# Sixteen more rows of expert products beside the making of gates, parked in DRAM, and gate sums two groups behind their one-hots

## The chip, the cores and the metric

One core of one Trainium2 chip runs the whole program. The metric is the device time of one execution in microseconds (us); lower is better. TensorE (PE) does the matrix products, VectorE (DVE), ScalarE (ACT) and GpSimd (POOL) the rest; SyncE (SP), ACT and POOL issue DMAs.

## The reference

Two transformer blocks run one after the other on 512 tokens of width 1024. The change lies in the last part of the second, a mixture of 16384 experts (128 x 128 keys), of which each token takes 128 (8 heads x 16):

```
sc = einsum(q, subkeys); vals, ids = top_k(sc, 16)          # two halves per head
cand = vals0 + vals1;  top, pos = top_k(cand, 16);  idx = expert numbers
g = softmax(top)
u = u_tab[idx]; a = einsum('chkd,cd->chk', u, x)            # 128 per token
wgt = g * gelu(a)
out = einsum('chk,chkd->cd', wgt, v_tab[idx])
```

## The kernel before, in words

The first 128 tokens take their experts by gathering rows of `u_tab` and `v_tab` (`gather`: 256 indirect DMAs of 512 KB issued by POOL, one long DVE operation for each). The other 384 tokens (`ND`) go through all 16384 experts densely, in 128 rows of 128 experts:

- `ustep(r)` makes row r of the first product: 24 matmuls of 128 x 384 over the transposed table `put`, in three terms of split precision, then a gelu on ACT into a slot of X, a ring of 38 slots in SBUF (`xrow`).
- `vstep(r)` multiplies row r by its gates (`gmul`), splits it in a high and a low part (`gmul`, `split`) and adds it into six PSUM banks by 18 matmuls of 128 x 512 over `pv`.
- Weights come as 512 KB tiles `wraw` on SP's queue, three buffers; ACT casts the high part `whi`, DVE subtracts the low part `wlo` (`wsplit`), one row ahead.

The gates of the 384 tokens are made before any `vstep` can run. `choice` yields small pieces of work, each with a cost: for each block of 128 tokens `chosen` and `weigh` (top 16 of the candidates, softmax, transposes), then `gates_of`: 16 groups of 8 tokens. A group is four DVE operations (two one-hots `o2`, `wh`, two products `wl`, `wh`) and two sums; a sum is 8 fp16 products of 128 x 128 on PE into a bank and one ACT copy into `sg`. Three sums fill an `sg` tile of 12 tokens (two buffers), which a DMA on ACT's queue writes to the DRAM table G. G is read back 8 rows at a time on SP's queue (`ring`).

Order of the work: nothing is scheduled at run time. `LEAD` = 37 rows of `ustep` come ahead of the first `vstep`; during them each of the 8 calls of `do` in a row adds `PACE0` to a debt, and pieces of `choice` are written into the streams until their costs have paid it (`tick`). Then rows of `ustep` and `vstep` alternate (PACE1, PACE2), with the choice for the first 128 tokens and the gather as the paced work, and when `ustep` has run out `vstep` goes on alone (PACE3). In `gates_of` the sums of a group are written after the DVE operations of the next one (a list `lag` that holds one group), and the three tiles of a group have two buffers each.

Of the kernel before, what the change touches and what calls it, by code (L numbers as in the profile page):

```python
# [10 lines left out]
F32 = mybir.dt.float32  # L11
F32R = mybir.dt.float32r
F16 = mybir.dt.float16
I32 = mybir.dt.int32
U32 = mybir.dt.uint32
AF = mybir.ActivationFunctionType
# [13 lines left out]
ND = 384  # L30
TB = 12
NB = ND // TB
GR = 8
GS = 32768.0

NX1, NX2 = 30, 8
LEAD = 37
NLAST = 11

PACE0, PACE1, PACE2, PACE3 = 0.85, 0.27, 0.21, 0.15  # L40

C_ANW, C_FNW, C_GNW, C_CW, C_AOG, C_COG, C_CW2, C_CT, C_N1, C_N2, C_FIN, C_N = 0, 8, 16, 17, 65, 69, 73, 85, 93, 101, 109, 117
R_ALOG, R_DTB, R_FB, R_SNK, R_QG, R_KG, R_IF, R_N = 0, 4, 8, 16, 24, 88, 152, 184
# [85 lines left out]
class Kern:  # L129
# [61 lines left out]
    def weights(self):  # L191
        a = self.a
        w = [a["wi"][i] for i in range(12)]
        for f in range(4):
            w += [a["wi"][16 + f], a["wi"][20 + f]]
        w += [a["wi"][24 + f] for f in range(4)]
        w += [a["wi"][12 + f] for f in range(4)]
        w += [a["wo"][h, k] for h in range(2) for k in (2, 3, 0, 1)]
        w += [a["wgu"][f, i] for f in range(NFF) for i in range(2)]
        w += [a["wd"][h, k] for h in range(2) for k in range(NFF // 2)]  # L200
        w += [a["wi2q"][k] for k in range(4)]
        w += [a["wi2k"][k] for k in range(2)]
        for f in range(4):
            w += [a["wi2b"][i + f] for i in (4, 8, 0)]
        w += [a["wo2"][h, k] for c in ((2, 3), (0, 1)) for h in range(2) for k in c]
        self.lim = len(w) + 2
        w += [a["wq"][f] for f in range(16)]
        self.lov = set()
        n = len(w)
        w += [a["put"][e] for e in range(LEAD)]  # L210
        for e in range(128):
            if e + LEAD < 128:
                w.append(a["put"][e + LEAD])
            w.append(a["pv"][e * 128:e * 128 + 128])
        self.lov.update(range(n, len(w)))
        self.wl, self.wraw, self.wsp, self.wi, self.w3 = w, [], [], 0, None
# [1493 lines left out]
    def peer(self):  # L1710


        nc, tc, a = self.nc, self.tc, self.a
        V, S, G = nc.vector, nc.scalar, nc.gpsimd
        hi, lo = self.h2
        with ExitStack() as es:
# [6 lines left out]
            av = self.tl(qp, [128, 128], F32)  # L1723
            self.i1T, self.i2T, self.ghT, self.glT = [self.tl(qp, [128, ND, 2], F16) for _ in range(4)]
            iota = self.tl(qp, [128, 128], F16)
            self.G = self.tl(self.dr, [128 // GR, 128, NB, GR, TB], F32)
            ub = [self.bank("gx") for _ in range(2)]
            with tc.tile_pool(name="q1", bufs=1, side="right") as q1:
                vals = self.tl(q1, [128, 4, 16, 16], F32)
                ids = self.tl(q1, [128, 4, 16, 16], U32)  # L1730
                with tc.tile_pool(name="q2", bufs=2, side="right") as q2:
# [12 lines left out]
                    for f in range(16):  # L1744
                        p = self.first[f][0] if f < 3 else self.proj512(hi, lo, 0)
                        qT = self.tl(q2, [128, T], F32, "qT", bufs=5)
                        S.copy(qT, p)
                        if f == 3:

                            for n in range(2):  # L1750
                                pb = self.bank("pj")
                                for j in range(4):
                                    k = n * 4 + j
# [13 lines left out]
                    r0 = len(pend) - 1  # L1767
# [4 lines left out]
                q3 = gp.__enter__()  # L1772
                work = self.choice(q1, q3, vals, ids, iota)

                def tick(pace):
                    self.due += pace
                    while self.due > 0:
                        c = next(work, None)
                        self.due = self.due - c if c else -1e9
                self.chose0 = False  # L1780
                ready = False
                for r in range(r0, LEAD):
                    self.ustep(hi, lo, r, ub, lambda: tick(PACE0 if not ready else PACE1))
                    if r == LEAD - 1:
                        for _ in range(0 if ready else 10**6):
                            if next(work, None) is None:
                                break
                    if not ready and (self.due < -1e6 or r == LEAD - 1):

                        ready = True  # L1790
                        gp.__exit__(None, None, None)
                        self.due = 0.0
                        rp = es.enter_context(tc.tile_pool(name="rp", bufs=2, reuse_waits="tile"))
                        self.ring(rp, 0)
                        gat = self.gather(qp, hm, ga, av)

                        def rest():
                            yield from self.chosen(q1, 0, vals[:, 0], ids[:, 0])
                            for x in self.late:
                                yield from x  # L1800
                            self.chose0 = True
                            yield from gat
                        work = rest()
# [2 lines left out]
                self.split(rp, 0)  # L1806
                k = 0
                while not self.chose0:
                    self.ustep(hi, lo, LEAD + k, ub, lambda: tick(PACE1))
                    self.vstep(rp, k, vb, lambda: tick(PACE1))  # L1810
                    k += 1
            for k in range(k, 126):
                if k + LEAD < 128:
                    self.ustep(hi, lo, LEAD + k, ub, lambda: tick(PACE2))
                pace = PACE2 if k + LEAD < 128 else PACE3
                self.vstep(rp, k, vb, lambda: tick(pace))
                if k == 128 - NLAST:
                    self.preload()
# [1 line left out]
                pass  # L1820
            self.finish(rp, ga, vb)

    def xrow(self, r):
        s = r % (NX1 + NX2)
        return self.X[0][:, s] if s < NX1 else self.X[1][:, s - NX1]

    def ring(self, rp, g):

        if g == 0:
            self.grows = []  # L1830
        t = self.tl(rp, [128, NB, GR, TB], F32, "gt", bufs=2)
        self.nc.sync.dma_start(t, self.G[g])
        self.grows.append(t)

    def gmul(self, rp, r):
# [9 lines left out]
    def preload(self):  # L1845

        nc = self.nc
        live = {r % (NX1 + NX2) for r in range(128 - NLAST, 128)}
        self.rowf = []
# [48 lines left out]
    def ustep(self, hi, lo, r, ub, do=lambda: None):  # L1898

        p = ub[r % 2][:, :ND]  # L1900
        self.prod(p, self.nextw(), (hi, lo), slice(128, 512), 8, do)
        self.nc.scalar.activation(self.xrow(r), p, AF.Gelu_apprx_tanh)  # L1902

    def vstep(self, rp, r, vb, do):

# [42 lines left out]
    def gates_of(self, q3, t, iota):  # L1948

        nc, V, S = self.nc, self.nc.vector, self.nc.scalar  # L1950
        lag = []

        def sums(n, o2, wh, wl):
            ps = self.bank("pj")
            for j in range(4):
                o = slice(j * 128, j * 128 + 128)
                self.mm(ps[:, o], o2[:, j], wh[:, j], True, False)
                self.mm(ps[:, o], o2[:, j], wl[:, j], False, True)
            q = n * 4 % TB
            if q == 0:  # L1960
                self.stage = self.tl(q3, [128, 128, TB], F32, "sg", bufs=2)
            S.activation(self.stage[:, :, q:q + 4].rearrange("p e j -> p j e"), ps.rearrange("p (j e) -> p j e", j=4),  # L1962
                         AF.Copy, scale=1.0 / GS)
            if q + 4 == TB:
                b = n * 4 // TB
                nc.scalar.dma_start(self.G[:, :, b].rearrange("g p r t -> p g (r t)"),
                                    self.stage.rearrange("p (g r) t -> p g (r t)", r=GR))
        GT = 8
        b2 = iota.rearrange("p (a b) -> p a b", b=2).unsqueeze(1).to_broadcast([128, GT, 64, 2])
        v4 = lambda ap: ap.rearrange("p t (a b) -> p t a b", b=2)  # L1970
        for n in range((t - 1) * 16, t * 16):
            o2, wh, wl = [self.tl(q3, [128, GT, 128], F16, tag, bufs=2) for tag in ("o2", "wh", "wl")]
            bt = lambda ap: ap[:, n * GT:n * GT + GT].unsqueeze(2).to_broadcast([128, GT, 64, 2])
            V.tensor_tensor(v4(o2), b2, bt(self.i2T), op=OP.is_equal)
            yield 0.66
            V.tensor_tensor(v4(wh), b2, bt(self.i1T), op=OP.is_equal)
            yield 0.66
            V.tensor_tensor(v4(wl), v4(wh), bt(self.glT), op=OP.mult)
            yield 0.66
            V.tensor_tensor(v4(wh), v4(wh), bt(self.ghT), op=OP.mult)  # L1980
            lag.append((n, o2, wh, wl))
            for m in range(2 if len(lag) > 1 else 0):
                sums(lag[0][0] * 2 + m, *[x[:, m * 4:m * 4 + 4] for x in lag[0][1:]])
                if m == 0:
                    yield 0.66
            if len(lag) > 1:
                lag.pop(0)
            else:
                yield 0.66
        for m in range(2):  # L1990
            sums(lag[0][0] * 2 + m, *[x[:, m * 4:m * 4 + 4] for x in lag[0][1:]])

    def gather(self, qp, hm, ga, av):
        nc, a = self.nc, self.a
# [181 lines left out]
```

## Time and profile before

| | |
|---|---|
| median of 3 runs | 2405.67 us (2398.84 to 2410.49) |
| the profiled execution | 2407.29 us, its span 2405.5 us |
| busy share of the span | PE 94%, DVE 68%, ACT 37%, POOL 33% |
| mean granted TensorE clock | 0.966 of full speed |
| DMA | 438.07 MB, 182 GB/s over the span |

Busy shares are means over stages with different limits, so a change of one stage is read from rows of that stage. PE matmuls are pipelined and their ends modelled, so the time of one row of products is read from the distance between equal instructions, not from their durations. "DMA share" is the mean busy share of the 16 DMA engines; a granted clock of 1.00 is 2.4 GHz, 0.5 is 1.2 GHz.

### The profile page before, as it was taken

What the parts mean: (1) busy time and instruction counts of PE and PEld (TensorE: products, weight loads), DVE (VectorE), ACT (ScalarE), POOL (GpSimd) and SP (SyncE); (2) the same over time, 40 slices, a digit from 0 to 9 for tenths busy, and PEclk for the clock granted to TensorE, in tenths of its full rate; (3) what the DMA queues carried; (4) which work ended last, traced back from release to release, by engine and by line L of the source; (5) the groups of instructions that cost most, each with busy time, mean ns of one, the idle gap of its engine ahead of it and who ended that gap; (6) DMA issues with size and microseconds to landing.
All of it is one profiled execution on the core that took longest, in us unless ns stands there. A gap on an engine that the chain in (4) does not pass through costs nothing.

```text
span 2405.5 us, 31911 instructions
## 1 busy us (share of the span) xinstructions
PE 2257.5 (94%) x12063; PEld 1948.3 (81%) x12063; DVE 1639.1 (68%) x3031; ACT 897.0 (37%) x1386; POOL 800.8 (33%) x519
## 2 busy tenths in 40 slices
PE   7898999999999998999968678999999999999998
PEld 6888777877778876778857668899999999999887
DVE  6865345465640266775897887778888788888865
ACT  4442423332222242443327565333333333333332
POOL 3553201555554353443100000234344343434300
PEclk9899889999999999999989899999999999999999
DMA  3122100365643221122226466698999999899954
GB/s 123 56 78 73 36 1 1 123 216 195 209 162 111 88 88 53 62 105 89 75 75 184 136 189 206 237 339 321 338 326 335 321 334 328 316 325 326 344 200 161
DMA packets 186647, 438.07 MB, mean 182 GB/s; under 512 B 89215, under 2 KB 90135, under 8 KB 184317
## 3 DMA queue, kind: packets, MB, share of 16 engines
q1 hardware_dynamic: 82172, 272.79, 32.3%
q0 software_dynamic: 37312, 135.20, 16.4%
q10 hardware_dynamic: 67008, 28.05, 4.4%
q8 instruction: 94, 1.54, 0.3%
q14 instruction: 61, 0.49, 0.1%
HBM read 405.22 MB, written 30.70 MB: 181 GB/s over the span
## 4 chain that ended last, share of the span: by engine, by line
PE 74%; DVE 15%; ACT 5%; DMA 3%; issue 2%; POOL 1%; SPq 0%; ACTq 0%; DVEq 0%; POOLq 0%
PE pj L161 42%; PE gx L161 25%; PE hold L161 5%; DMA u<-sg 2%; PE gx L185 2%; DVE w L634 2%; DVE wlo L234 1%; ACT whi L232 1%; ACT sg L1962 1%; DVE w L768 1%; DVE cmu L2108 1%; DVE cmu L2103 0%; DMA wraw<-in_wi_dram 0%; POOL alo L343 0%; DVE w L632 0%
## 5 line engine op out<-in xcount | busy, mean ns | idle before, releaser
L232 ACT CAST whi<-wraw 128x1024 fp32r<-128x1024 f32 x400 | 420.1, 1051 | 342.9 <-issue 147.9
L234 POOL TENSOR_TENSOR wlo<-wraw,whi 128x1024 fp32r<-128x1024 f32 x135 | 353.2, 2618 | 380.1 <-ACT whi L232 376.0
L234 DVE TENSOR_TENSOR wlo<-wraw,whi 128x1024 fp32r<-128x1024 f32 x265 | 329.9, 1245 | 196.4 <-ACT whi L232 194.1
L161 PE MATMUL gx<-alo,whi 128*128 128x384 f32 x1024 | 352.4, 344 | 0.0
L161 PE MATMUL gx<-ahi,whi 128*128 128x384 f32 x1024 | 351.1, 343 | 0.0
L2010 POOL DMA_INDIRECT gr<-in_pu_dram,u x128 | 152.0, 1187 | 577.2 <-DVE u L2133 351.4
L161 PE MATMUL pj<-ahi,whi 128*128 128x512 f32 (+2 forms) x1000 | 321.8, 362 | 4.5 <-ACT ahi L339 4.2
L161 PE MATMUL pj<-alo,whi 128*128 128x512 f32 (+2 forms) x1000 | 313.3, 353 | 0.0
L2010 POOL DMA_INDIRECT gr<-in_pv_dram,u x128 | 157.7, 1232 | 233.3 <-DVE u L2029 174.0
L161 PE MATMUL gx<-ahi,wlo 128*128 128x384 f32 x1024 | 214.2, 349 | 18.9 <-DVE wlo L234 18.9
L161 PE MATMUL pj<-ahi,wlo 128*128 128x512 f32 (+2 forms) x1000 | 210.1, 354 | 2.2 <-DVE wlo L234 2.2
L161 PEld LDWEIGHTS pj<-ahi,whi 128*128 128x128 f32 x1000 | 176.0, 193 | 37.3 <-issue 7.5
L161 PEld LDWEIGHTS gx<-ahi,wlo 128*128 128x128 f32 x1024 | 185.1, 195 | 21.8 <-DVE wlo L234 21.8
L161 PE MATMUL pj<-whi,eh 128*128 128x512 f32 x512 | 199.9, 390 | 0.0
L161 PE MATMUL pj<-wlo,eh 128*128 128x512 f32 x512 | 199.2, 389 | 0.0
L161 PEld LDWEIGHTS gx<-ahi,whi 128*128 128x128 f32 x1024 | 196.2, 192 | 3.6
L161 PEld LDWEIGHTS gx<-alo,whi 128*128 128x128 f32 x1024 | 196.1, 191 | 3.5
L161 PEld LDWEIGHTS pj<-alo,whi 128*128 128x128 f32 x1000 | 174.9, 192 | 23.8
L161 PEld LDWEIGHTS pj<-ahi,wlo 128*128 128x128 f32 x1000 | 165.2, 192 | 29.1 <-DVE wlo L234 2.6
L1902 ACT ACTIVATE u<-gx 128x384 f32<-128x384 f32 x128 | 63.5, 496 | 320.2 <-PE gx L161 319.7
L161 PE MATMUL pj<-whi,el 128*128 128x512 f32 x512 | 179.1, 390 | 0.0
L2029 DVE SCALAR_TENSOR_TENSOR u<-gr,u,u 128x1024 f32<-128x1024 f32 x128 | 163.9, 1281 | 2.5 <-DMA gr<-in_pv_dram,u 1.6
(472 smaller groups left out, 3872.2 us busy)
## 6 DMA issues: line engine op xcount, KB each, us to landing
wraw<-in_put_dram SPq DMA_DIRECT2D x128, 512.0 KB
wraw<-in_pv_dram SPq DMA_DIRECT2D x128, 512.0 KB
nu<-in_adaw_dram SPq DMA_DIRECT2D x48, 512.0 KB
u<-sg ACTq DMA_DIRECT2D x32, 768.0 KB
gt<-u SPq DMA_DIRECT2D x16, 1536.0 KB
wraw<-in_wgu_dram SPq DMA_DIRECT2D x44, 512.0 KB
wraw<-in_wi_dram SPq DMA_DIRECT2D x28, 512.0 KB
wraw<-in_wd_dram SPq DMA_DIRECT2D x22, 512.0 KB
```

Of the source, the lines that this page charges most:

```text
L161: self.nc.tensor.matmul(out, l, r, start=start, stop=stop)
L185: self.nc.tensor.transpose(out, in_, self.ident[:n, :n])
L232: self.nc.scalar.copy(hi, raw)
L234: (self.nc.vector if i in self.lov else self.nc.gpsimd).tensor_tensor(lo, raw, hi.bitcast(F32), op=OP.subtract)
L634: V.scalar_tensor_tensor(o, pad[:, t:t + TA], cw(t), o, op0=OP.mult, op1=OP.add)
L768: V.tensor_tensor(t, X[:, 0:i, 0:i].rearrange("p j c -> p c j"), A[:, i:i + 1, 0:i].to_broadcast([np_, i, i]), op=OP.mult)
L1902: self.nc.scalar.activation(self.xrow(r), p, AF.Gelu_apprx_tanh)
L1962: S.activation(self.stage[:, :, q:q + 4].rearrange("p e j -> p j e"), ps.rearrange("p (j e) -> p j e", j=4), AF.Copy, scale=1.0 / GS)
L2010: G.indirect_dma_start(out=u, out_offset=None, in_=a[items[i][0]], in_offset=bass.IndirectOffsetOnAxis(ap=self.idx[:, items[i][1]:items[i] ...
L2029: V.scalar_tensor_tensor(ga, u, wv[:, s:s + 1], ga, op0=OP.mult, op1=OP.add)
L2108: V.tensor_tensor(x[:, :, 0:n], x[:, :, 0:n], x[:, :, n:2 * n], op=OP.add)
```

## The change

`NSP` = 16 rows are put ahead of the lead: 53 rows of `ustep` now come before the first `vstep`. The first 16 go to slots of X and from there to a DRAM tile `xd` by a DMA on ACT's queue, so that their slots serve the next rows. The order of the `vstep`s is turned by 16: rows 16 to 127 first, rows 0 to 15 last, and G is read in that order. The 16 parked rows come back by DMAs on SP's queue, one at each of the first 16 steps that have no `ustep`. The sums of a group now follow by two groups instead of one, with three buffers for its tiles, and the costs per call of `do` are lower in the lead and higher after it.

```diff
+NSP = 16
-PACE0, PACE1, PACE2, PACE3 = 0.85, 0.27, 0.21, 0.15
+PACE0, PACE1, PACE2, PACE3 = 0.56, 0.30, 0.22, 0.17
...
-        w += [a["put"][e] for e in range(LEAD)]
-        for e in range(128):
-            if e + LEAD < 128:
-                w.append(a["put"][e + LEAD])
+        w += [a["put"][e] for e in range(NSP + LEAD)]
+        for k in range(128):
+            if NSP + LEAD + k < 128:
+                w.append(a["put"][NSP + LEAD + k])
+            e = (NSP + k) % 128
             w.append(a["pv"][e * 128:e * 128 + 128])
...
+            self.xd = self.tl(self.dr, [NSP, 128, ND], F32)
...
-                for r in range(r0, LEAD):
+                for r in range(r0, NSP + LEAD):
...
             for k in range(k, 126):
-                if k + LEAD < 128:
-                    self.ustep(hi, lo, LEAD + k, ub, lambda: tick(PACE2))
-                pace = PACE2 if k + LEAD < 128 else PACE3
+                both = NSP + LEAD + k < 128
+                if both:
+                    self.ustep(hi, lo, NSP + LEAD + k, ub, lambda: tick(PACE2))
+                elif k + LEAD < 128:
+                    nc.sync.dma_start(self.xrow(k + LEAD), self.xd[NSP + LEAD + k - 128])
+                pace = PACE2 if both else PACE3
                 self.vstep(rp, k, vb, lambda: tick(pace))
...
-        self.nc.sync.dma_start(t, self.G[g])
+        self.nc.sync.dma_start(t, self.G[(g + NSP // GR) % (128 // GR)])
...
-        self.nc.scalar.activation(self.xrow(r), p, AF.Gelu_apprx_tanh)
+        x = self.xrow(r - NSP if r >= NSP else r)
+        self.nc.scalar.activation(x, p, AF.Gelu_apprx_tanh)
+        if r < NSP:
+            self.nc.scalar.dma_start(self.xd[r], x)
...
-            o2, wh, wl = [self.tl(q3, [128, GT, 128], F16, tag, bufs=2) for tag in ("o2", "wh", "wl")]
+            o2, wh, wl = [self.tl(q3, [128, GT, 128], F16, tag, bufs=3) for tag in ("o2", "wh", "wl")]
...
-            for m in range(2 if len(lag) > 1 else 0):
+            for m in range(2 if len(lag) > 2 else 0):
...
-            if len(lag) > 1:
+            if len(lag) > 2:
                 lag.pop(0)
...
-        for m in range(2):
-            sums(lag[0][0] * 2 + m, *[x[:, m * 4:m * 4 + 4] for x in lag[0][1:]])
+        for x in lag:
+            for m in range(2):
+                sums(x[0] * 2 + m, *[y[:, m * 4:m * 4 + 4] for y in x[1:]])
+                yield 0.1
```

On ACT, in the middle of the gates of the third block, before the change (`sg` is a copied sum, `u<-gx` a gelu, `whi` the cast of the next row's weights, the DMA writes an `sg` tile to G):

```order
L232 CAST whi_11384<-wraw_11185 128x1024
L1962 ACTIVATE sg_11359<-pj_11394 128x4x128
L1966 DMA u_8628<-sg_11359 128x16x96
L1962 ACTIVATE sg_11417<-pj_11408 128x4x128
L1962 ACTIVATE sg_11417<-pj_11432 128x4x128
L1962 ACTIVATE sg_11417<-pj_11445 128x4x128
L1966 DMA u_8628<-sg_11417 128x16x96
L1962 ACTIVATE sg_11478<-pj_11469 128x4x128
L1962 ACTIVATE sg_11478<-pj_11483 128x4x128
L1902 ACTIVATE u_8617<-gx_8629 128x384
L232 CAST whi_11498<-wraw_11299 128x1024
```

and with it:

```order
L1911 ACTIVATE u_8617<-gx_8630 128x384
L235 CAST whi_11397<-wraw_11282 128x1024
L1973 ACTIVATE sg_11390<-pj_11418 128x4x128
L1973 ACTIVATE sg_11390<-pj_11431 128x4x128
L1977 DMA u_8629<-sg_11390 128x16x96
L1973 ACTIVATE sg_11467<-pj_11458 128x4x128
L1911 ACTIVATE u_8617<-gx_8631 128x384
L235 CAST whi_11470<-wraw_11335 128x1024
L1973 ACTIVATE sg_11467<-pj_11482 128x4x128
L1973 ACTIVATE sg_11467<-pj_11508 128x4x128
L1977 DMA u_8629<-sg_11467 128x16x96
```

Six sums stood between two casts, now three. Over the whole lead the 96 sums stood beside 19 rows of `ustep` and now stand beside 27; of the other rows ahead of the last sum, 14 were there before (rows 0 and 1 among them), and 22 are now.

On ACT beside the first choosing, where the parked rows are made, each gelu is now followed by a DMA to `xd`:

```order
L1911 ACTIVATE u_8617<-gx_8631 128x384
L1913 DMA u_8628<-u_8617 128x384
L235 CAST whi_9947<-wraw_9857 128x1024
L2154 ACT_TABLE_LOAD
L2154 ACTIVATE ctv_9682<-ctv_9682 128x128
L1911 ACT_TABLE_LOAD
L1911 ACTIVATE u_8617<-gx_8630 128x384
L1913 DMA u_8628<-u_8617 128x384
L235 CAST whi_10002<-wraw_9906 128x1024
```

Nothing of this sort stood between a gelu and the cast behind it. On SP, from the first `vstep` without a `ustep`, with the change (`gt` is the read of G):

```order
L1821 DMA u_8617<-u_8628 128x384
L224 DMA wraw_18374<-in_pv_dram 128x1024
L1821 DMA u_8617<-u_8628 128x384
L224 DMA wraw_18407<-in_pv_dram 128x1024
L1821 DMA u_8617<-u_8628 128x384
L1840 DMA gt_18431<-u_8629 128x3072
L224 DMA wraw_18442<-in_pv_dram 128x1024
```

At these 16 steps SP issued a `put` tile and a `pv` tile before; now it issues a parked row of 196,608 bytes and a `pv` tile.

## Rows read from the trace of the kernel before

**Rows 1.** Windows: busy us (count) of PE, PEld, DVE, ACT, POOL; clock, DMA share, GB/s.

```profile
1196.60:1249.00 52.40, 36.88 (x180) 34.59 (x179) 51.13 (x239) 15.26 (x22) 0.00 (x0) 0.90 0.24 79
1249.00:1322.00 73.00, 54.56 (x436) 48.52 (x437) 59.73 (x126) 45.34 (x49) 0.00 (x0) 0.86 0.60 166
...
1350.00:1467.00 117.00, 88.60 (x769) 77.41 (x767) 91.97 (x133) 78.54 (x86) 0.00 (x0) 0.92 0.68 185
...
1196.60:1467.00 270.40, 197.81 (x1466) 176.45 (x1465) 229.95 (x583) 148.81 (x172) 0.00 (x0) 0.89 0.53 148
1560.00:2245.00 685.00, 685.00 (x3472) 625.15 (x3471) 558.50 (x689) 244.94 (x339) 280.05 (x232) 1.00 0.92 329
2246.00:2307.00 61.00, 61.00 (x271) 50.53 (x270) 53.17 (x63) 22.53 (x30) 14.44 (x12) 1.00 0.83 297
```

**Rows 2.** Chain that ended last, steps with both products: start us, us, what.

```profile
2155.72 4.64 PE gx L161 x26
2164.02 4.65 PE gx L161 x26
```

**Rows 3.** Timeline of PE, steps of the second product alone: start us, us.

```profile
2246.79 0.39 PE L161 MATMUL gx<-whi,eh 128*128 128x512 f32 x1
...
2250.87 0.39 PE L161 MATMUL gx<-whi,eh 128*128 128x512 f32 x1
```

**Rows 4.** Chain, in the gates of the last blocks (1350 to 1467 us).

```profile
1356.30 6.01 DMA u<-sg
...
1366.65 8.11 DMA u<-sg
...
1387.06 7.19 DMA u<-sg
...
1395.21 1.11 ACT sg L1962
1396.64 0.94 ACT whi L232
1397.60 1.23 DVE wlo L234
```

**Rows 5.** Waits in 1196 to 1470 us: us in total, times, longest.

```profile
PEld L161 <- DVE wh L1980: 58.5, 34, 10.0
...
DVE wlo L234 <- ACT whi L232: 32.7, 18, 4.7
ACT sg L1962 <- DMA u<-sg: 21.3, 9, 3.8
```

**Rows 6.** Timeline of DVE in the gates: a group's first operation, and the next group's.

```profile
1356.44 0.68 DVE L1974 TENSOR_TENSOR o<-u,u 128x1024 f16<-128x1024 f16 x1
...
1359.10 0.69 DVE L1974 TENSOR_TENSOR o<-u,u 128x1024 f16<-128x1024 f16 x1
```

**Rows 7.** Timeline of PE in the gates: 8 products of a sum, from first to next.

```profile
1353.30 0.23 PE L161 MATMUL pj<-wh,o 128*128 128x128 f16 x1
...
1353.72 0.42 PE L161 MATMUL gx<-alo,whi 128*128 128x384 f32 x1
```

**Rows 8.** Timeline of ACT in the gates: two gelus eleven rows apart, one DMA issue.

```profile
1353.79 0.55 ACT L1902 ACTIVATE u<-gx 128x384 f32<-128x384 f32 x1
...
1361.02 0.37 ACTq L1966 DMA_DIRECT2D u<-sg  x1
...
1463.31 0.54 ACT L1902 ACTIVATE u<-gx 128x384 f32<-128x384 f32 x1
```

**Rows 9.** Groups of DVE, ACT and of the gather, 1100 to 1550 us and later.

```profile
L234 DVE TENSOR_TENSOR wlo<-wraw,whi 128x1024 fp32r<-128x1024 f32 x52 | 63.7, 1225 | 48.2 <-ACT whi L232 48.0
L1962 ACT ACTIVATE sg<-pj 128x512 f32<-128x512 f32 x96 | 100.9, 1104 | 70.5 <-PE pj L161 44.4 <-DMA u<-sg 21.3 <-ACT sg L1962 4.8
...
L2029 DVE SCALAR_TENSOR_TENSOR u<-gr,u,u 128x1024 f32<-128x1024 f32 x128 | 163.9, 1281 | 2.5 <-DMA gr<-in_pv_dram,u 1.6
```

**Rows 10.** Tile `gt`: count, ns min/median/max, first and last start of `gmul`.

```profile
L1837 DVE TENSOR_TENSOR u<-u,gt x128: 497/552/558, 1490.9 to 2392.1; 128x384 f32<-128x384 f32 x128
```

More of the change, by code (lines that the diff above doesn't have):

```diff
@@ L1781, in peer @@
                 ready = False
-                for r in range(r0, LEAD):
+                for r in range(r0, NSP + LEAD):
                     self.ustep(hi, lo, r, ub, lambda: tick(PACE0 if not ready else PACE1))
-                    if r == LEAD - 1:
+                    if r == NSP + LEAD - 1:
                         for _ in range(0 if ready else 10**6):
@@ L1787, in peer @@
                                 break
-                    if not ready and (self.due < -1e6 or r == LEAD - 1):
+                    if not ready and (self.due < -1e6 or r == NSP + LEAD - 1):
                         ready = True
@@ L1808, in peer @@
                 while not self.chose0:
-                    self.ustep(hi, lo, LEAD + k, ub, lambda: tick(PACE1))
+                    self.ustep(hi, lo, NSP + LEAD + k, ub, lambda: tick(PACE1))
                     self.vstep(rp, k, vb, lambda: tick(PACE1))
@@ L1821, in peer, with xrow @@
             self.finish(rp, ga, vb)
-    def xrow(self, r):
-        s = r % (NX1 + NX2)
+    def xrow(self, k):
+        s = k % (NX1 + NX2)
         return self.X[0][:, s] if s < NX1 else self.X[1][:, s - NX1]
```

## The prediction

> **What bounds the kernel now.** I went from the stages to the waits. The windows by stretch come first [rows 1]. From 1560 us on PE is busy in the whole of each stretch at a granted clock of 1.00 (2.4 GHz): 685.00 of 685.00 us while both products run, 61.00 of 61.00 where the second runs alone. In the lead it is not: 197.81 of 270.40 us from 1196.60 to 1467.00. So the late part is worth what its rows of products cost, and the lead has 72.6 us in which PE stands still.
>
> The price of a row comes from the distance of equal instructions. A step with both products takes 2164.02 - 2155.72 = 8.30 us [rows 2], a step of the second alone 2250.87 - 2246.79 = 4.08 us [rows 3]. A row of `ustep` is the difference, 4.22 us.
>
> Why PE stands still in the lead differs by stretch. Beside the choosing, 1196.60 to 1249.00, DVE is busy 51.13 of 52.40 us: it is the bound [rows 1]. Beside the gates no engine is full: DVE 59.73 of 73.00 and 91.97 of 117.00 us, ACT 78.54 of 117.00. Two gelus eleven rows apart stand at 1353.79 and 1463.31, 9.96 us per row [rows 8]. The chain there goes round a loop [rows 4]: the write of an `sg` tile to G (6.01, 8.11, 7.19 us in three of its pieces), the copy of a sum that waited for that buffer, the cast `whi` behind it on ACT, `wlo` behind that on DVE, and from there by way of one-hots and sums to the next write. The waits say the same from the engines' side [rows 5]: PE's weight loads for `wh` 58.5 us in 34 times, `wlo` for the cast 32.7 us, a sum's copy for an `sg` buffer 21.3 us.
>
> **The change, part by part.**
>
> *Sixteen rows leave the late part.* After the lead 128 - 37 = 91 steps of the second product shared their time with a `ustep`, now 128 - 53 = 75 do; the steps of the second product stay 128. PE is full there, so this takes off 16 x 4.22 = 67.5 us. They are not free ahead of it: they come to the lead.
>
> *Sixteen rows more in the lead, lower pace.* By the order of PE, 8 of them land beside the choosing and 8 beside the sums (12 rows without sums become 20, leaving out rows 0 and 1, which stay where they were; 19 with sums become 27).
> Beside the choosing DVE is the bound and each row brings it one `wlo` of 1.225 us [rows 9]: 8 x 1.225 = +9.8 us. PE's 4.22 us a row lie beside it: it had 52.40 - 36.88 = 15.5 us free in that stretch alone.
> Beside the gates the 8 new `wlo` are 9.8 us of DVE work, for which it has 73.00 - 59.73 + 117.00 - 91.97 = 38.3 us of idle time: nothing if only the idle time is filled. The cover is the loop; if the loop goes, these 9.8 us count, and they are in the next figure. The stretch has two bounds. From above: G's tiles keep their pace. The two stretches are 190 us for 96 sums, and would be 190 us again: 7.0 us for each of 27 rows in place of 10.0 for 19. From below: the fullest engine sets it. A row then carries 96 / 27 = 3.56 sums, that is 1.78 groups. DVE: a group takes 1359.10 - 1356.44 = 2.66 us [rows 6], so 1.78 x 2.66 + 1.225 = 5.96 us. PE: a sum takes 1353.72 - 1353.30 = 0.42 us [rows 7], so 4.22 + 3.56 x 0.42 = 5.7 us. ACT: 3.56 copies of 1.10 us [rows 9], a gelu of 0.55 us, 1.19 issues of 0.37 us [rows 8] and a cast of 0.94 us [rows 4], 5.85 us. DVE is the fullest: 27 x 5.96 = 161 us, 29 us less than now. The three lie within 0.3 us of each other, so a stall of any one soon stops the others, and 161 us would need that none occurs.
>
> *The lag of two groups and the third buffer.* They take DVE's last products off PE's path: PE's sums then need one-hots that were ready a group, 2.66 us, earlier. That speaks to the 58.5 us of waits for `wh`, and to nothing else in the loop: write, copy, cast and `wlo` stand in it as before, and a copy still holds the cast behind it when it waits for a buffer. At the ends of blocks two groups of sums, four copies of 1.10 us, come one upon the other, where it was one group. I take a fifth of the 29 us, -6 us, nearer to the upper bound because the transfers in the chain are the loop's longest pieces. The lead: +9.8 - 6 = +4 us, with -19 us (9.8 - 29) and +19.6 us (all 16 `wlo`, nothing filled) as ends. The Trainium skill's DMA: Bandwidth & Descriptors (Anatomy of one DMA) fits a DMA, there one issued by GpSimd, with 2.0 us plus its bytes at 436 GB/s, by estimate 3.8 us for a tile of 128 x 16 x 96 words. The chain's pieces of 6.01 to 8.11 us differ from it, and the measurement decides; by the page the writes would hide, the whole 29 us would go, and the sum would be the first rival's.
>
> *The spill.* 16 DMA issues on ACT, 0.37 us each [rows 8], 5.9 us, in a stretch where ACT is busy 15.26 of 52.40 us [rows 1]: nothing. What is behind an issue there is a cast for a row that starts a row later; without that cover it would be the 5.9 us. The slots are rewritten 16 rows later, long after a transfer.
>
> *The way back and the paces.* G's turned order costs nothing. In the first 16 steps of the second product alone, SP issues a parked row ahead of each `pv` tile; its slot's last reader is a step old, so SP waits for little, and its weights run up to three tiles ahead. What may be short there is the rate. Now such a step moves 297 GB/s x 4.08 us = 1.21 MB at a DMA share of 0.83 [rows 1]. It will move 0.197 MB of parked row more, and by PACE3 0.17 for 0.15 (8 calls a step, 1.2 a gather) a gather of 0.524 MB 1.13 times in place of once, 0.07 MB more: 1.48 MB, 362 GB/s. The share says that 297 / 0.83 = 358 GB/s fills the engines (with both products 329 / 0.92 = 358 as well). So each of 16 steps is too long by 1%, 0.05 us: +1 us; the upper end is that such a mixture doesn't get past the 297 GB/s it has now, below as a rival. With both products PACE2 0.22 for 0.21 brings 2.93 gathers per step for 2.80, 329 x 8.30 = 2.73 MB + 0.07, 337 GB/s or 94%: covered. DVE there: 558.50 / 685.00 of 8.30 us = 6.8 us a step, and 0.13 x 1.281 = 0.17 us more [rows 1, 9]; in the steps of the second product alone 53.17 / 61.00 x 4.08 = 3.56 + 0.17 = 3.7 of 4.08 us: covered. The gather ends at step 118 in place of 106, still 9 steps from the end, so no tail of it stands behind PE.
>
> **The sum** is made against the profiled execution's 2407.29 us (span 2405.5 and 1.8 around it; 1.6 above the median): -67.5 + 9.8 - 6 + 1 = -62.7 us, 2344.6 us; I say **2345 us**.
>
> **The rivals.**
>
> *The lead becomes engine-bound.* With the lag, PE and ACT no longer wait for one-hots, and G's writes hide behind a longer stretch: 161 us for the gates. For it: the waits for `wh` are the longest of [rows 5]. Against it: the chain holds transfers of 6 to 8 us [rows 4]. Time: 2407.3 - 67.5 + 9.8 - 29 + 1 = 2322 us. The Trainium skill's fit for a DMA, above, speaks for this case.
>
> *The late part becomes bound by DMA.* If the steps of the second product alone get no more than their present 297 GB/s, 16 steps of 1.48 MB and 27 of 1.28 MB (without the parked row) until the gather ends take 80 + 116 = 196 us in place of 43 x 4.08 = 175: +20 us, 2365 us. For it: 362 GB/s is more than any stretch moves now. Against it: with both products the chip does move 329 GB/s.
>
> *Slower: G's writes take the lead.* 16 rows' weights and 16 parked rows share the DMA engines with the writes, and rows come more densely. Two `sg` buffers make one fill and one transfer a loop for two tiles, so each us that a write gets longer lengthens 32 tiles by half a us, 16 us in all; it holds ACT, so the cast, `wlo` and PE. To lose the 62.7 us and 12 more, writes of 6 to 8 us would have to grow by 4.7 us. From there on it is slower: 2419 us and more. Against it: the DMA share beside the gates is 0.60 and 0.68 [rows 1], and the new rows bring it at most to the 0.92 of the late part, where DVE still gets its weights in time.
>
> *The lag does nothing and the 16 `wlo` all count*, +19.6 us in the lead: 2360 us. It lies in the range of the forecast's own case.
>
> **The numbers.** A measurement of this kernel can tell about 0.5%, 12 us, from no change. Chances: the forecast with its own spread (2330 to 2362) 0.58; the engine-bound lead 0.18; the DMA-bound late part 0.11; G's writes 0.06; a gain eaten up to within 12 us by two of these together 0.07. The range that holds it 8 times in 10 reaches from the engine-bound lead, less a few us, to the DMA-bound late part with +19.6 us in the lead on top (2380): 2318 to 2380 us. Faster by over 0.5%: 0.87, within 0.07, slower 0.06.
>
> **What would show it.** Right: steps of 8.30 and 4.08 us unchanged, 75 and not 91 with both products; the first `gmul`, at 1490.9 us now [rows 10], some 4 us later (1472 to 1510); rows beside the gates at 6.7 to 7 us each; fewer waits for `wh` and as many for `sg` buffers as now; a higher granted clock in the lead. Wrong: a step of 4.5 us after the last `ustep` with gathers late (the DMA rival), rows of 6 us beside the gates (the engine-bound lead), `sg` writes of 11 us (the slower one), or a stall at the first step that reads a parked row.

## The result and the profile after

The changed kernel takes 2347.43 us (median of 4 runs, 2344.18 to 2353.3) where the kernel before takes 2406.64 us on the same chips: a ratio of 0.9761, 95% interval 0.9729 to 0.9792. The profiled execution's span is 2344.3 us, 61.2 us less than before.

The page's part 2 of the changed kernel, PE's busy tenths and the granted clock in 40 slices:

```profile
PE   7898999999999998998989899999999999999998
...
PEclk9899888999999999999999999999999999999999
```

The windows of the changed kernel (columns as in [rows 1]): the two stretches of gates, the lead as a whole, the steps with both products, and 70 us of the steps of the second product alone:

```profile
1256.00:1316.00 60.00, 59.26 (x500) 53.96 (x498) 55.21 (x100) 47.81 (x53) 0.00 (x0) 1.00 0.83 234
...
1344.50:1467.00 122.50, 118.29 (x990) 108.48 (x989) 102.89 (x146) 94.18 (x108) 0.00 (x0) 0.98 0.79 218
...
1560.00:2110.00 550.00, 549.13 (x2777) 499.84 (x2776) 456.94 (x565) 195.97 (x273) 238.37 (x195) 1.00 0.93 337
...
2140.00:2210.00 70.00, 69.50 (x299) 55.18 (x298) 58.40 (x78) 23.70 (x33) 18.22 (x18) 1.00 0.94 348
...
1196.60:1467.00 270.40, 249.76 (x1880) 232.04 (x1881) 243.59 (x578) 173.90 (x206) 0.00 (x0) 0.98 0.66 191
```

In the same 270.40 us of the lead PE now works 249.76 us where it worked 197.81 [rows 1]; beside the gates it is busy 177.55 of 182.50 us. The granted clock of the lead rose from 0.89 to 0.98. The waits there, 1196 to 1490 us, answer to [rows 5]:

```profile
DVE wlo L237 <- ACT whi L235: 25.9, 11, 5.8
...
ACT sg L1973 <- DMA u<-sg: 14.3, 13, 2.3
...
PEld L163 <- DVE wh L1991: 6.3, 9, 1.6
```

PE's waits for `wh` fell from 58.5 to 6.3 us, the others less; those for an `sg` buffer went from 21.3 us in 9 times to 14.3 us in 13, where the prediction had them unchanged. The first `gmul`, by the tile of gates, answers to [rows 10]:

```profile
L1845 DVE TENSOR_TENSOR u<-u,gt x128: 495/552/561, 1484.3 to 2330.8; 128x384 f32<-128x384 f32 x128
```

So the span splits in two. From the start to the first `gmul`, 1490.9 became 1484.3 us: -6.6. From there to the end 914.6 became 860.0 us: -54.6. The prediction had +4 and -66.5. The sum, -61.2 for -62.7, hides that both parts were off. Of the -6.6 us, moreover, only 3.3 lie behind the third gelu of the lead (1196.6 us before, 1193.3 after); the rest lies ahead, where hardly anything was changed. And the experiments show that these -3.3 us are what is left of two much larger effects of opposite sign.

### The profile page after: what moved, and what is told of

It reads as the page before. It is cut to its first block, busy times and chain, and to the rows that moved or that the text cites. A ratio compares the mean times of both kernels' runs of the same rounds, so it can differ in the third digit from the quotient of the medians.

```text
span 2344.3 us, 31959 instructions
## 1 busy us (share of the span) xinstructions
PE 2245.6 (96%) x12063; PEld 1928.2 (82%) x12063; DVE 1634.3 (70%) x3031; ACT 894.6 (38%) x1386; POOL 794.0 (34%) x519
## 3 DMA queue, kind: packets, MB, share of 16 engines
q0 software_dynamic: 37312, 135.20, 16.5%
## 4 chain that ended last, share of the span: by engine, by line
PE 67%; DVE 20%; ACT 5%; issue 4%; DMA 2%; POOL 1%; ACTq 0%; SPq 0%; DVEq 0%; POOLq 0%
PE pj L163 39%; PE gx L163 23%; PE hold L163 4%; DVE wlo L237 3%; DVE w L637 2%; ACT whi L235 2%; PE gx L187 2%; DMA u<-sg 1%; DVE u L2042 1%; DVE u L1845 1%; DVE w L771 1%; DVE cmu L2121 1%; ACT sg L1973 1%; DVE w L635 1%; DVE gr L2034 0%
## 5 line engine op out<-in xcount | busy, mean ns | idle before, releaser
L2023 POOL DMA_INDIRECT gr<-in_pv_dram,u x128 | 149.8, 1171 | 246.1 <-DVE u L2042 186.0
L163 PE MATMUL gx<-ahi,wlo 128*128 128x384 f32 x1024 | 208.2, 342 | 15.3 <-DVE wlo L237 15.3
L163 PEld LDWEIGHTS gx<-ahi,whi 128*128 128x128 f32 x1024 | 194.4, 190 | 12.6 <-ACT whi L235 9.8
L163 PEld LDWEIGHTS gx<-ahi,wlo 128*128 128x128 f32 x1024 | 179.8, 190 | 18.5 <-DVE wlo L237 18.5
```

What stands on the lines that cost most here:

```text
L163: self.nc.tensor.matmul(out, l, r, start=start, stop=stop)
L2023: G.indirect_dma_start(out=u, out_offset=None, in_=a[items[i][0]], in_offset=bass.IndirectOffsetOnAxis(ap=self.idx[:, items[i][1]:items[i] ...
```

## The experiments

Two questions: what did the rows and the lag each do in the lead, and what makes the steps of the second product alone slower than PE. Kernels of one group ran on one chip beside the kernel before.

### The change again, and its two halves apart

> The changed kernel once more, as the yardstick of this group of runs: 2347 us by all theories, 2.4% under the kernel before.

Measured: 2351.15 us, ratio 0.9774 (0.9756 to 0.9793).

The lag alone, on the kernel before (all of the change in `gates_of`, of which the main lines are shown):

```diff
-            o2, wh, wl = [self.tl(q3, [128, GT, 128], F16, tag, bufs=2) for tag in ("o2", "wh", "wl")]
+            o2, wh, wl = [self.tl(q3, [128, GT, 128], F16, tag, bufs=3) for tag in ("o2", "wh", "wl")]
...
-            for m in range(2 if len(lag) > 1 else 0):
+            for m in range(2 if len(lag) > 2 else 0):
...
```

> The kernel before with only the lag of two groups and the third buffer; pace, rows and order as before. Theory: the lag takes away PE's waits for wh by itself, the gates' stretch of 190 us loses 6 to 12 us, 2395 to 2400 us. Rival one: at the old pace the loop of G's writes, copy, cast and wlo sets it, and nothing is won (2406 us). Rival two: the lag is most of what the lead can give (29 us), 2378 us.

Measured: 2378.7 us, ratio 0.9894 (0.9874 to 0.9914), 26.5 us less than before: the second rival, not the theory. The reverse edit on the changed kernel (lag of one, two buffers; the rows and the paces stay):

```diff
-            o2, wh, wl = [self.tl(q3, [128, GT, 128], F16, tag, bufs=3) for tag in ("o2", "wh", "wl")]
+            o2, wh, wl = [self.tl(q3, [128, GT, 128], F16, tag, bufs=2) for tag in ("o2", "wh", "wl")]
...
-            for m in range(2 if len(lag) > 2 else 0):
+            for m in range(2 if len(lag) > 1 else 0):
...
```

> The changed kernel with the sums one group behind and two buffers, all else as changed. Theory: the sixteen rows and the thinner pace fill PE by themselves, and the lag gives 5 to 10 us of the change: 2352 to 2357 us. Rival one: the lag gives nothing at this pace, 2347 us. Rival two: without it PE's stalls come back as they were and the 8 rows beside the gates are not covered: 2375 us and more.

Measured: 2372.85 us, ratio 0.9861 (0.9839 to 0.9882), 21.7 us above the change: near the second rival's 2375, and clearly more than the theory's 5 to 10 us. The stretch from the first to the last copy of a sum shows where it lies. One window each, columns as before (PE's busy time first, DVE's third); first the kernel before:

```profile
1257.00:1471.00 214.00, 163.86 (x1305) 144.80 (x1304) 171.39 (x327) 135.87 (x152) 0.00 (x0) 0.89 0.61 169
```

the lag alone:

```profile
1257.00:1445.00 188.00, 158.99 (x1307) 142.45 (x1306) 170.08 (x327) 133.72 (x154) 0.00 (x0) 0.91 0.69 192
```

the changed kernel without the lag:

```profile
1267.00:1487.00 220.00, 201.46 (x1590) 182.53 (x1589) 183.48 (x339) 153.00 (x176) 0.00 (x0) 0.97 0.68 193
```

and the changed kernel:

```profile
1258.00:1467.00 209.00, 197.05 (x1595) 181.56 (x1593) 183.83 (x340) 152.20 (x177) 0.00 (x0) 0.98 0.73 206
```

With the lag alone the same work of DVE, some 170 us, takes 188 us in place of 214: DVE is busy 90% of it. With the rows alone the stretch grows by 6 us (214 to 220) for 285 more matmuls and 12 more DVE operations: those rows do go into the gaps. With both, the gaps are gone and the rows cost: 188 to 209 us, PE busy 94%. The first `gmul` of the four starts at 1490.9, 1463.0, 1508.6 and 1484.3 us; counted from the third gelu of the lead (1196.6, 1196.4, 1202.1, 1193.3 us), since the part ahead of it, in which the edits add no more than the DMA issues of two parked rows, moved by some us from trace to trace, the lead is 294.3, 266.6, 306.5 and 291.0 us. So **the lag alone is worth -27.7 us, the rows alone cost +12.2, and the rows on top of the lag cost +24.4**.

Where in the lead these sizes lie is read from the copies of the sums, of which 32 stand in a first stretch of gates and 64 in a second. The times are those of the first and the last start. The kernel before, then the lag alone, the rows alone and the changed kernel:

```profile
L1962 ACT ACTIVATE sg<-pj x32: 1065/1100/1182, 1257.4 to 1315.3; 128x512 f32<-128x512 f32 x32
L1962 ACT ACTIVATE sg<-pj x64: 1057/1102/1183, 1349.4 to 1469.4; 128x512 f32<-128x512 f32 x64
...
L1962 ACT ACTIVATE sg<-pj x32: 1072/1111/1178, 1257.2 to 1305.0; 128x512 f32<-128x512 f32 x32
L1962 ACT ACTIVATE sg<-pj x64: 1067/1114/1175, 1340.9 to 1442.9; 128x512 f32<-128x512 f32 x64
...
L1973 ACT ACTIVATE sg<-pj x32: 1072/1108/1187, 1267.4 to 1327.8; 128x512 f32<-128x512 f32 x32
L1973 ACT ACTIVATE sg<-pj x64: 1067/1112/1192, 1366.1 to 1484.4; 128x512 f32<-128x512 f32 x64
...
L1973 ACT ACTIVATE sg<-pj x32: 1088/1118/1172, 1258.5 to 1312.2; 128x512 f32<-128x512 f32 x32
L1973 ACT ACTIVATE sg<-pj x64: 1067/1114/1180, 1351.6 to 1464.2; 128x512 f32<-128x512 f32 x64
```

| us | before | lag alone | rows alone | changed |
|---|---|---|---|---|
| beside the choosing (third gelu to first copy, and between the stretches) | 94.9 | 96.7 | 103.6 | 104.6 |
| the two stretches of gates | 177.9 | 149.8 | 178.7 | 166.3 |
| last copy to first `gmul` | 21.5 | 20.1 | 24.2 | 20.1 |

The lag acts on the gates, -28.1 us, and on little else. The rows cost 8 to 9 us beside the choosing with the lag or without it; beside the gates they cost 0.8 us without it and 16.5 us with it.

### What in the lag did it

The third buffer without the lag, on the kernel before (without the change of `lag`):

```diff
-            o2, wh, wl = [self.tl(q3, [128, GT, 128], F16, tag, bufs=2) for tag in ("o2", "wh", "wl")]
+            o2, wh, wl = [self.tl(q3, [128, GT, 128], F16, tag, bufs=3) for tag in ("o2", "wh", "wl")]
```

> The kernel before with three buffers for the tiles of a group, sums still one group behind. Theory: the 27 us of the lag come from the place of the sums in PE's stream, and DVE hardly waited for buffers (2.5 us): no difference, 2402 to 2406 us. Rival: the third buffer is what helps: 2379 us.

Measured: 2408.25 us, ratio 1.0006 (0.9993 to 1.0018). The buffer alone is nothing: the gain needs the other place of the sums in PE's stream. That place with two buffers only was not tried.

A third `sg` buffer instead, on the kernel before:

```diff
-                self.stage = self.tl(q3, [128, 128, TB], F32, "sg", bufs=2)
+                self.stage = self.tl(q3, [128, 128, TB], F32, "sg", bufs=3)
```

> The kernel before with a third sg buffer, so that a copy never waits for a write to G of two tiles ago. What the prediction held: the writes are the longest pieces of the loop that sets the gates, so without these waits (21 us) the lead loses 10 to 20 us, 2386 to 2396 us. Theory after the run with the lag alone: the loop is PE waiting for one-hots, the writes only fill what it leaves, 2400 to 2406 us.

Measured: 2387.87 us, ratio 0.9913 (0.989 to 0.9936). This is the prediction's reading of the loop, not the later one: without waits for the writes the stretch takes 193 us for 214. Its window, its copies as above (155.7 us in the two stretches of gates, where the kernel before takes 177.9), and the waits for `wh` in it (1262 to 1454 us):

```profile
1262.00:1455.00 193.00, 157.71 (x1310) 138.96 (x1308) 171.05 (x327) 136.17 (x152) 0.00 (x0) 0.93 0.67 188
```

```profile
L1962 ACT ACTIVATE sg<-pj x32: 1067/1106/1174, 1262.5 to 1314.5; 128x512 f32<-128x512 f32 x32
L1962 ACT ACTIVATE sg<-pj x64: 1068/1104/1194, 1348.7 to 1452.4; 128x512 f32<-128x512 f32 x64
```

```profile
PEld L161 <- DVE wh L1980: 36.6, 40, 2.9
```

So the two readings fit as halves of one loop. The write holds a copy, the copy the cast, the cast `wlo`, `wlo` the one-hots, the one-hots PE, and PE the copies of the next write. Cutting it at the writes takes away 21 us, cutting it at the one-hots 26. The two can't add up, since only 43 us lie between the 214 us and DVE's 171 us of work, and after either cut DVE is busy 89 or 90% of what is left. Both cuts at once were not tried. In the run with the lag alone the copies still wait 21.3 us for writes, as much as before [rows 5], though the stretch is 26 us shorter.

### What the pace is worth

The changed kernel, with the gather placed as in the next section, and the old pace of 0.85 in the lead:

```diff
-PACE0, PACE1, PACE2, PACE3 = 0.56, 0.30, 0.22, 0.17
+PACE0, PACE1, PACE2, PACE3 = 0.85, 0.30, 0.22, 0.17
```

> The changed kernel with the gather in the gap, and with the old pace of 0.85 in the lead: the gates stand beside 19 rows again, the other rows of the lead come behind the last sum. Theory: with the lag, the gates then take DVE's own time (152 us, as with the lag alone), and the rows behind them cost their full 4.22 us of PE, which takes back what they save later: about 2365 us, 25 us above the version with the gather in the gap. Rival: the pace is worth nothing, the rows fill the gaps wherever they stand: 2342 us.

Measured: 2386.94 us, ratio 0.9924 (0.9905 to 0.9943), 45 us above the version with the new pace, which ran on another chip. My figure was too low by the theory's own pieces: the lag alone had given 2378.7; against it the late part is 63.5 us shorter (914.6 to 851.1), and the lead 16 x 4.22 = 67.5 us longer if each row costs a full step: 2383 us (in the traces it is 72.9 us longer). The rows stand behind the last sum; here are the copies of the sums and the `gmul`s of that run:

```profile
L1974 ACT ACTIVATE sg<-pj x96: 1067/1118/1177, 1255.7 to 1443.8; 128x512 f32<-128x512 f32 x96
```

```profile
L1846 DVE TENSOR_TENSOR u<-u,gt x128: 545/551/555, 1534.4 to 2372.0; 128x384 f32<-128x384 f32 x128
```

The sums end 20 us earlier than in the changed kernel, and the first `gmul` comes 50 us later. Rows are cheap only ahead of the last sum, beside the choosing and the gates, so the number of rows and the pace are one choice. That is also what more or fewer rows say, 24 and then 8, both on the version with the gather placed as in the next section, with paces to fit:

```diff
-NSP = 16
+NSP = 24
...
-PACE0, PACE1, PACE2, PACE3 = 0.56, 0.30, 0.22, 0.17
+PACE0, PACE1, PACE2, PACE3 = 0.485, 0.30, 0.22, 0.19
```

> 24 rows parked in place of 16, gather in the gap, pace 0.485 so that the lead's work is again spread over all its rows, PACE3 0.19 so that the gather ends in time. Theory: beside the gates PE is full (118 of 122 us), so 8 rows more cost there what they save later, and only those beside the choosing win: 2336 to 2344 us, no difference from 2342. Rival: rows ahead still cost 1 to 2 us each and save 4.22: 2320 to 2326 us.

Measured: 2348.3 us, ratio 0.9768 (0.9749 to 0.9786). No gain; the lead (from the third gelu) is 311.4 us, 20 more than the 291.2 us of the same version with 16 rows, and the late part 833.0 us, only 18.9 us less than the 851.9 of the next section, not 8 x 4.22 = 34 less. The steps of the second product alone mostly keep their pace: 54 of them, until 2296 us, take 4.07 us in the mean. The next one takes 10.96 us; there (2298 to 2325 us) ACT's cast waits for a tile of weights:

```profile
ACT whi L235 <- DMA wraw<-in_pv_dram: 6.8, 1, 6.8
```

And the 67 steps with both products take 563.4 us, where the first 67 of the version with 16 rows take 557.9. Why, was not tried apart.

```diff
-NSP = 16
+NSP = 8
...
-PACE0, PACE1, PACE2, PACE3 = 0.56, 0.30, 0.22, 0.17
+PACE0, PACE1, PACE2, PACE3 = 0.665, 0.30, 0.22, 0.17
```

> 8 parked rows in place of 16, gather in the gap, pace 0.665 so that the lead's work is spread over all its rows. Theory: with PE full beside the gates at 16 rows, the first 8 rows are the cheap ones: the lead is 10 to 16 us shorter than with 16, the late part 34 us longer, 2360 to 2366 us. Rival: all rows are alike at some 2 us: 2360 is the same by that; told apart from it by the gates' stretch, 152 to 158 us by the theory (DVE's bound), 160 by the rival.

Measured: 2365.5 us, ratio 0.9826 (0.9805 to 0.9847). The lead is 278.3 us and the late part 888.4 us; the two stretches of gates, by the copies of their sums (to the end of the last copy of each), are 158 us, at the edge of the theory's range. From 0 to 8 to 16 to 24 rows (always with the lag) the lead grows by 11.7, 12.9 and 20.2 us: the first 16 cost 1.5 us each, the next 8 2.5.

### The steps of the second product alone

In the changed kernel 44 of these steps, from the second on until the gather ends, take 185.9 us, 4.22 each in place of 4.08. DVE's timeline there, and ACT's cast `eh` from it:

```profile
2142.27 0.55 DVE L1845 TENSOR_TENSOR u<-u,gt 128x384 f32<-128x384 f32 x1
2143.48 0.56 DVE L1851 TENSOR_TENSOR el<-u,eh 128x384 fp32r<-128x384 f32 x1 [0.66 <-ACT eh L1847]
2144.44 1.23 DVE L237 TENSOR_TENSOR wlo<-wraw,whi 128x1024 fp32r<-128x1024 f32 x1 [0.39 <-ACT whi L235]
2145.58 1.22 DVE L2034 SCALAR_TENSOR_TENSOR gr<-gr,u 128x1024 f32<-128x1024 f32 x1
2146.72 0.08 DVE L2034 DVE_READ_ACCUMULATOR gr<-gr,u 128x1 f32 x1
2146.72 0.56 DVE L1845 TENSOR_TENSOR u<-u,gt 128x384 f32<-128x384 f32 x1
```

```profile
2142.93 0.51 ACT L1847 CAST eh<-u 128x384 fp32r<-128x384 f32 x1 [2.98 <-DVE u L1845]
```

One step from `gmul` to `gmul` is 4.45 us, 3.4 of it work and 1.05 two waits for ACT: DVE hands the row to ACT's cast `eh` and has nothing to do until it is back, then waits for `whi`, which stands behind `eh`. The operation that could fill the first wait, the gather's, stands behind `wlo`. With PACE3 at 0.15 the eight calls of a step paid 1.2, exactly one gather, always at a call between `gmul` and `split`; 0.17 makes the debt drift, so that in most steps it falls due behind `wlo`. The edit pays a step's pace at its first two calls:

```diff
-                self.vstep(rp, k, vb, lambda: tick(pace))
+                calls = iter((4 * pace, 4 * pace, 0, 0, 0, 0, 0, 0))
+                self.vstep(rp, k, vb, (lambda: tick(pace)) if both else (lambda: tick(next(calls))))
```

> The paced gather of the steps without a ustep is written between gmul and split only (the first two calls of do pay for the whole step). Theory: with the gather behind wlo, DVE waits 0.66 us for the cast eh and 0.4 us for the cast whi in each step, so a step is a loop of DVE and ACT of 4.45 to 4.50 us, longer than PE's 4.08; with the gather in the gap the step of DVE is some 3.4 us and PE sets 4.08 again. Steps of 4.08 us, 6 to 8 us faster than the change (2340 us). Rival, DMA sets these steps (348 GB/s there): steps stay at 4.2 us in the mean, time as the change.

Measured: 2341.88 us, ratio 0.9744 (0.9729 to 0.976), beside 2351.15 us of the change on the same chip. DVE's timeline of this version:

```profile
2145.50 0.55 DVE L1846 TENSOR_TENSOR u<-u,gt 128x384 f32<-128x384 f32 x1
2145.97 1.22 DVE L2035 SCALAR_TENSOR_TENSOR gr<-gr,u 128x1024 f32<-128x1024 f32 x1
2147.11 0.08 DVE L2035 DVE_READ_ACCUMULATOR gr<-gr,u 128x1 f32 x1
2147.45 0.61 DVE L1852 TENSOR_TENSOR el<-u,eh 128x384 fp32r<-128x384 f32 x1 [0.25 <-ACT eh L1848]
2148.44 1.23 DVE L237 TENSOR_TENSOR wlo<-wraw,whi 128x1024 fp32r<-128x1024 f32 x1 [0.38 <-ACT whi L235]
2149.58 0.55 DVE L1846 TENSOR_TENSOR u<-u,gt 128x384 f32<-128x384 f32 x1
```

The step is 4.08 us, PE's own, and the stretch from the first `gmul` to the end fell from 860.0 to 851.9 us. DMA was not the limit; a window of the same version, 100 us with the parked rows coming back:

```profile
2110.00:2210.00 100.00, 100.00 (x443) 82.66 (x442) 88.45 (x121) 38.06 (x52) 34.56 (x30) 1.00 0.96 360
```

The same from the other side, the changed kernel with the reload left out (the DMA of a parked row at each of 16 steps; the second product then works on old rows there):

```diff
-                elif k + LEAD < 128:
-                    nc.sync.dma_start(self.xrow(k + LEAD), self.xd[NSP + LEAD + k - 128])
```

> The changed kernel without the DMAs that bring the parked rows back (the last 16 rows of the second product are then made from other rows' slots). Theory: the steps without a ustep stay at 4.45 us, since DVE and ACT set them. Rival: the added 0.197 MB a step set them, and the first 16 fall to 4.08 us.

Measured: 2355.81 us in one run, and steps as in the changed kernel, though only 300 GB/s were moved from 2120 to 2180 us, where the changed kernel moved 344 in the same 60 us of its steps (2110.4 to 2170.4 us):

```profile
2147.59 0.56 DVE L1843 TENSOR_TENSOR u<-u,gt 128x384 f32<-128x384 f32 x1
2148.81 0.56 DVE L1849 TENSOR_TENSOR el<-u,eh 128x384 fp32r<-128x384 f32 x1 [0.66 <-ACT eh L1845]
...
2152.05 0.55 DVE L1843 TENSOR_TENSOR u<-u,gt 128x384 f32<-128x384 f32 x1
```

### A last try, and the best version

The version with the gather in the gap once more, and the same with a lower PACE1 for the first steps of both products:

> The version with the gather in the gap again, as the yardstick of this group: 2342 us, 2.6% under the kernel before.

Measured: 2340.02 us, ratio 0.9739 (0.9721 to 0.9756).

```diff
-PACE0, PACE1, PACE2, PACE3 = 0.56, 0.30, 0.22, 0.17
+PACE0, PACE1, PACE2, PACE3 = 0.56, 0.25, 0.22, 0.17
```

> The same with PACE1 0.25 for 0.30: the pieces of the choice for the first 128 tokens lie thinner over the first steps with both products, of which one takes 12.6 us in the traces with 0.30. Theory: that stall of 4 us goes, and the gather still ends two steps or more ahead of the last: 2338 us. Rival: the pieces only move, 2342 us.

Measured: 2343.96 us, ratio 0.9753 (0.9737 to 0.9769): the rival. The longest of the first steps is 10.33 us in place of 12.6, but the late part is 857.5 us for 851.9; the pieces only moved. The version with the gather in the gap stays the best: 2341.88 and 2340.02 us in two groups, 2.6% below the kernel before, and 6 to 11 us below the two medians of the change (2347.43 and 2351.15), with the stretch behind the first `gmul` shorter by 8 us in its traces.

## Why the prediction was right, step by step

**The price of a row and what 16 of them save.** Near in the steps with both products: 75 of them from 1484.3 to 2107.1 us, 8.30 us each. In the steps of the second product alone the term was mis-sized: "DVE there: ... 3.7 of 4.08 us: covered". That compared DVE's busy time with the step. What counts is DVE's chain with ACT, 4.45 us with the gather in the wrong place. It cost the 8 us that the edit gave back; the late part lost 54.6 us in place of 66.5. The rest of the difference, some 4 us, lies in the steps with both products: the first 75 of them took 618.5 us in the kernel before, 8.25 us in the mean and not the 8.30 of the one step that was read, and take 622.8 us now. Why they are longer, the runs do not show.

**The sixteen rows in the lead.** The +9.8 us were worked out for the 8 rows beside the choosing, and there they came true: 94.9 us became 104.6. For the 8 rows beside the gates the prediction had two cases, the idle time filled or DVE's bound. Without the lag they did fill the idle time (+0.8 us); with it they cost 16.5 us, since there was little idle time left.

**The lag of two groups.** This is the step that failed, hidden by the sum: "That speaks to the 58.5 us of waits for `wh`, and to nothing else in the loop ... I take a fifth of the 29 us, -6 us". Alone it is worth 27.7 us. With one link of the loop cut, the links behind it moved too, and the gates fell to the next bound. By the prediction's own terms DVE's time beside 19 rows is 48 x 2.66 + 19 x 1.225 = 151 us, and the gates of the run with the lag alone, by their copies, take 149.8, about that. In the change the gates with their 27 rows lost 11.6 us, 177.9 to 166.3, twice the -6: -28.1 by the lag, +16.5 by the rows. The forecast of the lead, +4 for a measured -3.3, was near by luck: two large effects that it had not seen nearly cancelled.

**The spill and the way back.** Costed at nothing and +1 us. The reload is shown to cost nothing measurable: without it the late part is 860.6 us, with it 860.0. The spill was not tried by itself.

**The rivals.** The engine-bound lead, which had a chance of 0.18, came true in its mechanism: beside the gates PE is busy 97% of the time. It did so by its own sign too. Read as in [rows 8], rows there are 6.10 us apart (it had 6, the forecast's own case 6.7 to 7); of the changed kernel, two gelus 17 rows apart:

```profile
1354.08 0.53 ACT L1911 ACTIVATE u<-gx 128x384 f32<-128x384 f32 x1
...
1457.72 0.53 ACT L1911 ACTIVATE u<-gx 128x384 f32<-128x384 f32 x1
```

The time was not 2322 for two reasons. The 190 us that the prediction set against the bound of 161 are 12 more than the 177.9 us from the first copy to the last in the two stretches, so that by the copies some 17 us were to be had and not 29, and 11.6 were had. And the late part saved 12 us less. The Trainium skill's fit (DMA: Bandwidth & Descriptors, Anatomy of one DMA) had stood for this rival with an estimate of 3.8 us a write; the page gives it for DMAs issued by GpSimd, and these are ACT's. By the rows of after the writes in the chain still took 5.62 to 6.85 us, so the estimate doesn't hold for these writes:

```profile
1399.73 5.62 DMA u<-sg
...
1445.10 6.85 DMA u<-sg
```

The DMA-bound late part is refuted as a cause; its symptom, steps of more than 4.08 us while the gather lasts, came from DVE and ACT. G's writes as a slower mechanism: refuted, those in the chain did not get longer (6.01 to 8.11 us before).

## What to carry to other kernels

When several engines wait for each other in a ring, don't share the idle time out among the waits: work out the fullest engine's own time, and allow for a cut of the ring at one place to go most of the way there, as both cuts did here (177.9 us of gates became 149.8 and 155.7, with DVE's own time at 151); then what is added to the freed stretch is no longer covered by idle time. Two edits on one stretch are not additive, and the order in which they are tried decides which of them seems to pay. And a paced filler belongs where its engine would otherwise wait for another: read an engine's cover from the chain of its operations in a step, not from its busy share.

## What the runs showed of the hardware

DMA moved 360 GB/s over 100 us at a busy share of 0.96 while PE was busy for all 100 us; the prediction had put the limit at 358 by the quotient of two rows, and the same quotient here is 375. A row handed from DVE to ACT and back, 0.51 us of work on ACT, kept DVE idle for 0.66 us where no other operation stood between, and a cast queued behind it for another 0.39. And with PE fuller in the lead its clock was higher: granted 0.89 with 197.81 us busy of 270.40 before, 0.98 with 249.76 us after.
